# Two halves of a weight tile interleaved element by element, and all large buffers 32 bytes lower

## The chip, the cores and the metric

The kernel runs on one core of one Trainium2 chip. The metric is the device time of one execution in microseconds. Three runs of the kernel before took 1808.83 to 1810.48 us, median 1809.73. A separate execution was profiled; its trace is what the prediction reads.

## The reference, cut to what matters

Two requests of 512 tokens by 1024 features (`x_prompt`, `x_sample`) pass through the same two layers and a last RMSNorm, all in float32. Each layer is `x = x + Mixer(RMSNorm(x))`:

```python
def diff_attention(h, w_in, ..., subln_g, w_out, lambda_init):
    proj = h @ w_in                       # 1024 x 8192
    q, k, v, gate = jnp.split(proj, ...)  # q, k rotated; 16 heads of 128, v: 8 heads of 256
    ...
    p = jax.nn.softmax(s, axis=-1)        # two maps per head
    a = p[:, :, 0] - lam * p[:, :, 1]
    o = rms_norm(a @ v, subln_g, SUBLN_EPS) * (1.0 - lambda_init) * jax.nn.silu(gate)
    return o @ w_out                      # 2048 x 1024

def bidir_retention(h, w_in, ..., subln_g, w_out):
    proj = h @ w_in                       # 1024 x 6144
    q, k, v, gate = jnp.split(proj, ...)  # q, k rotated in pairs; 8 heads of 128, v of 256
    o = rms_norm(o_f + o_b, subln_g, SUBLN_EPS) * jax.nn.silu(gate)
    return o @ w_out
```

`o_f` and `o_b` are decayed, unnormalised attention forwards and backwards in time. Most of the work is in `h @ w_in` of the two layers.

## The kernel before

**Precision by two halves.** A float32 operand is split into a high part (a cast to `fp32r`, made by ScalarE, `hi_of`, the operation at L400) and a low part (the operand minus its high part, made by VectorE, `lo_of`, L403). A product is then three matmuls into the same PSUM bank: high by high, high by low, low by high (`PASSES`).

**Projections.** `h @ w_in` is computed unit by unit, a unit being 256 columns of the weight matrix. Each unit uses a scheme with seven block products (`P1` to `P7`, in the order `SEQ`) instead of eight. For each, `prep` takes blocks of the weights (`raw`, loaded by DMA) or sums of such blocks (`st`, L558), splits them into halves in the ring `ws`, and `product` multiplies them by a prepared operand `Bop` that stands in the buffers `b..` and in slots of one large buffer, `arena`. There are two kinds of unit:

- *pair* (q, k and gates): the weights are the stationary operand, 128 columns at a time; the moving operand has 512 columns. One product is 12 matmuls (four row blocks by three passes, L599). Its two halves stand in one `ws` tile of 1024 elements per partition, the high half in the first 512, the low half in the last 512.
- *wide* (v): the weights are the moving operand, 256 columns; the halves stand in two `ws` tiles (L609).

The ring `ws` has seven places. `projections` prepares products as far ahead of the one that is multiplied as the ring has places for (a pair product takes one, a wide one two). What the products leave in PSUM is combined, rotated or gated, split again and stored to DRAM scratch.

**Mixers and output.** Attention (scores L1116, exponentials L1134, transposes L1161, the product with v L1181) and retention (L1315, L1339, L1359, L1367) load these back. The output product (`out_step`, L891) has its own halves of weights in `ws`; its steps are mixed among the mixers' ones, and the second layer's first output products among the projections.

**Order.** All operations are recorded with a cost and their dependences in `Plan`, which then lays them out: the queue of each engine (PE, ACT = ScalarE, DVE = VectorE, POOL = GpSimd, SP) is in the order in which they would start by these costs. Dependences go by buffer or by part of a buffer. Semaphore waits are added afterwards by the framework, by the memory that operations touch.

**Places in SBUF.** Four pools follow each other in each partition: small tiles (`sm`, each rounded up to 32 bytes), large buffers and tables (`cp`), the arena (`ar`), the rings (`wk`). `view` sends every tile whose size is no multiple of 16 elements to `sm`. So the size of `sm` sets where all that follows begins. In the kernel before, the buffers `b..` begin at 32 modulo 256 bytes, the slots of the arena at 32, 96 or 160 (`shift` of 0, 16 or 32 elements), the rings at 224. In every matmul but the transposes and warming ones, weights and moving operand differ by 64 or 192 modulo 256.

**Constants.** `mhalf` (four times -0.5) and `minus1` (one -1.0) are exponents for GpSimd's power operation: `mhalf` in `norm_cols` (L823), `row_norm`, `x_norm` (L1018); `minus1` for the reciprocals in `combine` (L1144).

The lines that the change is about, as they stand before (L574 to L581):

```python
if self.wide:
    a, b = ws_t([P, 4, n]), ws_t([P, 4, n])
    hi, lo = ((lambda: a.t), a), ((lambda: b.t), b)
else:
    s = ws_t([P, 2, 4, n])
    hi, lo = ((lambda: s[:, 0]), (s, 0)), ((lambda: s[:, 1]), (s, 1))
hi_of(4 * n, lambda: self.like(hi[0]()), src[0], [src[1]], [hi[1]])
lo_of(4 * n, lambda: self.like(lo[0]()), src[0], lambda: self.like(hi[0]()), [src[1], hi[1]], [lo[1]])
```

Of the kernel before, what the change touches and what calls it, by code (L numbers as in the profile page):

```python
# [12 lines left out]
ALU = mybir.AluOpType  # L13
AX = mybir.AxisListType

P = 128
# [3 lines left out]
NT = S // P  # L20
# [233 lines left out]
def trunk_kernel(  # L254
# [7 lines left out]
    nc = tc.nc  # L262
# [4 lines left out]
    sm = ctx.enter_context(tc.tile_pool(name="sm", bufs=1))  # L267
# [12 lines left out]
    def view(pool, tag, i, size, shape, dt=F32):  # L280


        if size % 16 and pool in (cp, wk):
            pool = sm
        if (tag, i) not in places:
            places[tag, i] = pool.tile([P, size], F32, tag=f"{tag}{i}", name=f"{tag}_{i}", bufs=1)
        n = math.prod(shape[1:])
        t = places[tag, i][0:shape[0], 0:n]
        if dt != F32:
            t = t.bitcast(dt)  # L290
        if len(shape) == 3:
            t = t.rearrange("p (a b) -> p a b", a=shape[1])
        elif len(shape) == 4:
            t = t.rearrange("p (a b c) -> p a b c", a=shape[1], b=shape[2])
        return t

    def work(tag, shape, bufs, dt=F32, name=None):
        size = SIZE.get(tag, shape[1])
        return Buf(plan, tag, bufs, lambda i: view(wk, tag, i, size, shape, dt))
# [24 lines left out]
    def const(shape, tag, dt=F32, size=None):  # L324
        return Buf(plan, tag, 1, lambda i: view(cp, tag, i, size or math.prod(shape[1:]), shape, dt))

    def ws_t(shape):
        return work("ws", shape, WS_BUFS, F32R)
# [4 lines left out]
    def st_t(shape, name="st"):  # L333
        return work("st", shape, 3, name=name)
# [13 lines left out]
    def col(n=1, tag="col", bufs=4):  # L348
        return work(tag, [P, n], bufs)
# [18 lines left out]
    def act(n, fn, r, w):  # L368
        plan.op("ACT", 0.1 + 0.00083 * n, fn, r, w)

    def dve(n, fn, r, w, wait=0.0):
        plan.op("DVE", 0.07 + 0.00104 * n, fn, r, w, wait=wait)

    def axpy(n, fn, r, w):

        plan.op("DVE", 0.13 + 0.00104 * n, fn, r, w)

    def pool(n, fn, r, w):
        plan.op("POOL", 0.15 + 0.0024 * n, fn, r, w)

    def evac(n, out, src, scale, r, w, each=0.00115):

        def fn(e):
            if e == "ACT":
                nc.scalar.activation(out(), src(), AF.Copy, scale=scale())  # L385
            else:
                nc.vector.tensor_scalar(out(), src(), scale(), None, op0=ALU.mult)
        plan.op(dict(DVE=0.07 + each * n, ACT=0.1 + 0.00092 * n), 0, fn, r, w)

    def pe(cost, fn, r, w, wait=0.0):  # L390
        plan.op("PE", cost, fn, r, w, wait=wait)

    def dma(out, in_, r, w, kb, eng=None):

        q = eng or nc.sync
        plan.op("SP" if eng is None else "ACT", 0.62, lambda: q.dma_start(out(), in_()), r, w, lands=2.0 + kb / 200.0,
                kb=kb, load=any(isinstance(k[0] if isinstance(k, tuple) else k, Buf) for k in w))

    def hi_of(n, dst, src, r, w):
        act(n, lambda: nc.scalar.copy(dst(), src()), r, w)  # L400

    def lo_of(n, dst, src, hi, r, w):
        dve(n, lambda: nc.vector.tensor_tensor(dst(), src(), hi().bitcast(F32), op=ALU.subtract), r, w)  # L403
# [1 line left out]

    ident = const([P, P], "ident")
    dma(lambda: ident.t, lambda: ident_in, [], [ident], 64, nc.scalar)
    mhalf = const([P, NT], "mhalf")
    dve(4, lambda: nc.vector.memset(mhalf.t, -0.5), [], [mhalf])
    minus1 = const([P, 1], "minus1")  # L410
    dve(1, lambda: nc.vector.memset(minus1.t, -1.0), [], [minus1])
    rows = work("m", [P, P], 4, name="rows")
    gcol = const([P, 28], "gcol")
    dve(1, lambda: nc.vector.memset(gcol[:, 20:21], D * EPS), [], [(gcol, 4)])
# [103 lines left out]
    class Unit:  # L518
# [32 lines left out]
        def prep(self, op):  # L551
            x = self.take
            n = 256 if self.wide else P

            def combine(a, b, fn):
                t = st_t([P, 4, n])
                out = ((lambda: self.like(t.t)), t)
                dve(4 * n, lambda: nc.vector.tensor_tensor(out[0](), a[0](), b[0](), op=fn), [a[1], b[1]], [t])  # L558
                return out
            if op == "P1":  # L560
                src = x(0, 0)
            elif op == "P2":
                src = x(0, 1)
            elif op == "P4":
                src = x(1, 1)
            elif op == "P5":
                src = self.s[1] = combine(x(1, 0), x(1, 1), ALU.add)
            elif op == "P6":
                src = self.s[2] = combine(self.s[1], x(0, 0), ALU.subtract)
            elif op == "P3":  # L570
                src = combine(x(0, 1), self.s[2], ALU.subtract)
            else:
                src = combine(x(0, 0), x(1, 0), ALU.subtract)
            if self.wide:  # L574
                a, b = ws_t([P, 4, n]), ws_t([P, 4, n])
                hi, lo = ((lambda: a.t), a), ((lambda: b.t), b)
            else:
                s = ws_t([P, 2, 4, n])
                hi, lo = ((lambda: s[:, 0]), (s, 0)), ((lambda: s[:, 1]), (s, 1))
            hi_of(4 * n, lambda: self.like(hi[0]()), src[0], [src[1]], [hi[1]])  # L580
            lo_of(4 * n, lambda: self.like(lo[0]()), src[0], lambda: self.like(hi[0]()), [src[1], hi[1]], [lo[1]])  # L581
            self.ops[op] = (hi, lo)
            if op == "P2" and self.early is not None:
                self.early, self.x = None, {}
# [226 lines left out]
    def norm_cols(sq, ps, guard):  # L811

        def fn():
            for t in range(2):
                nc.tensor.transpose(ps[:, t * P:(t + 1) * P], sq[:, t * P:(t + 1) * P], ident.t)
        pe(0.22, fn, [sq, ident], [ps])
        ss, rr = col(2, "css"), col(2, "crr", 9)
        for t in range(2):
            act(P + 120, lambda t=t: nc.scalar.activation(
                ps[:, 256 + t * P:256 + (t + 1) * P], ps[:, t * P:(t + 1) * P], AF.Copy, accum_out=ss[:, t:t + 1]),  # L820
                [(ps, t)], [(ps, 2 + t), (ss, t)])
        guard(ss)
        pool(200, lambda: nc.gpsimd.tensor_tensor(rr.t, ss.t, mhalf[:, 0:2], op=ALU.pow), [ss, mhalf], [rr])  # L823
        return rr

    def new_oT(g):
# [94 lines left out]
    def row_norm(g, t):  # L921

        ss, r = halves.pop((g, t)), col(1, "rsf", 4)
        pool(200, lambda: nc.gpsimd.tensor_tensor(r.t, ss.t, mhalf[:, 0:1], op=ALU.pow), [ss, mhalf], [r])
        return r


# [84 lines left out]
    def x_norm(g, t, late=()):  # L1012
        ss, r = col(1, "ssf", 12), col(1, "rsf", 4)
        jk = slot(16 + t % 2, [P, D])
        x = xnat[g, t]
        act(1250, lambda: nc.scalar.activation(jk.t, x.t, AF.Square, accum_out=ss.t), [x, *late], [jk, ss])
        pool(60, lambda: nc.gpsimd.tensor_scalar(ss.t, ss.t, 1.0 / D, EPS, op0=ALU.mult, op1=ALU.add), [ss], [ss])
        pool(200, lambda: nc.gpsimd.tensor_tensor(r.t, ss.t, mhalf[:, 0:1], op=ALU.pow), [ss, mhalf], [r])  # L1018
        evac(D, lambda: x.t, lambda: x.t, lambda: r.t, [x, r], [x], 0.00058)

    def x_source(layer, tiles, turn):
# [27 lines left out]
    for t in range(NT):  # L1049
        x_norm(1, t, [(Bop['B11', 3], 1)])  # L1050
# [31 lines left out]
    for i in range(2):  # L1082
        dve(16, lambda i=i: nc.vector.tensor_tensor(
            powers[:, :, 2 * i:2 * i + 2], powers[:, :, 2 * i:2 * i + 2], lr[:, i, :].unsqueeze(2).broadcast_to([P, NH, 2]),
            op=ALU.mult), [lr, powers], [powers])
# [52 lines left out]
    def combine(i):  # L1138

        p, sm, n = st[i]['p'], st[i - i % 2]['sm'], i % 2  # L1140
        rc, cc = col(tag="rc"), col(tag="cc")
        on, eng = (pool, nc.gpsimd) if i >= NT else (dve, nc.vector)
        if i >= NT:
            pool(200, lambda: nc.gpsimd.tensor_tensor(rc.t, sm[:, 2 + n:3 + n], minus1.t, op=ALU.pow),  # L1144
                 [(sm, (1, n)), minus1], [rc])
        else:
            dve(2, lambda: nc.vector.reciprocal(rc.t, sm[:, 2 + n:3 + n]), [(sm, (1, n))], [rc])
        on(100, lambda: eng.tensor_scalar(
            cc.t, sm[:, n:n + 1], rc.t, neglam.t, op0=ALU.mult, op1=ALU.mult), [(sm, (0, n)), rc, neglam], [cc])
        axpy(S, lambda: nc.vector.scalar_tensor_tensor(  # L1150
            p[:, 0, :], p[:, 1, :], cc.t, p[:, 0, :], op0=ALU.mult, op1=ALU.add), [p, cc], [p])
        if n:
            pool(40, lambda: nc.gpsimd.tensor_tensor(sm[:, 2:4], sm[:, 0:2], sm[:, 0:2], op=ALU.mult), [sm], [sm])
# [237 lines left out]
    def final_norm(g, t, i, half, n, key, end):  # L1391
# [14 lines left out]
        if not end:  # L1406
            return
        r = row_norm(g, t)
        for h, (z, part) in enumerate(zs):
            if final or h == 0:  # L1410
# [123 lines left out]
```

## Time and profile before

| | |
|---|---|
| runs | 1808.83, 1809.73, 1810.48 us |
| span of the profiled execution | 1807.0 us, 2.7 us under the median of the runs |
| granted TensorE clock | 0.999 of full speed |
| PE busy | 1794.9 us, 10299 matmuls |
| DVE busy | 1477.1 us |
| ACT busy | 895.1 us |
| POOL busy | 169.5 us |
| DMA | 328.81 MB, mean 182 GB/s |

A time outside of the span is what the execution spends before the first and after the last instruction. The stages in the trace: the start and the first layer's projections up to about 635 us, attention to about 1020 us, the second layer's projections to about 1500 us, retention to the end, with overlaps. Matmuls overlap in the array: the mean length of one in a group (392 ns, say) is longer than the distance from one to the next, so lengths of unbroken runs divided by their number of matmuls tell what one costs. `PEld` are the loads of the stationary operand, which run beside matmuls. A group is named by line, engine, operation and `out<-in`; behind the bar stand the busy time, the mean length in ns and the idle time before, with what ended it.

### The profile page before, as it was taken

The numbers are of one execution on the slowest core, as the hardware profiler recorded it, in microseconds if no ns is written. First come the engines' busy times: TensorE is split into PE (matmuls) and PEld (weight loads), VectorE is DVE, ScalarE is ACT, GpSimd is POOL, SyncE is SP. The second block draws the span as 40 slices with busy tenths as digits, with TensorE's granted clock in tenths as the row PEclk, the third lists the DMA queues.
The fourth block names the chain that finished last, engine by engine and source line by source line (L and its number), as shares of the span: only waits on it lengthen the run. The fifth ranks groups of instructions, "written<-read, shape, count | busy, mean of one in ns | idle before, by whom it ended". The sixth has DMA issues, their size and how long they took to land.

```text
span 1807.0 us, 27780 instructions
## 1 busy us (share of the span) xinstructions
PE 1794.9 (99%) x10299; PEld 1558.1 (86%) x10299; DVE 1477.1 (82%) x2319; ACT 895.1 (50%) x1856; POOL 169.5 (9%) x323
## 2 busy tenths in 40 slices
PE   9999999999999999999999999999999999999998
PEld 6789889898988888888888888898989898888887
DVE  7958787778699888888888897787887967888887
ACT  7753444433434565554555866444434355444346
POOL 1000000000000022222322300000000000111113
PEclk9999999999999999999999999999999999999999
DMA  6444455555545685444554524464657559765662
GB/s 217 134 126 137 161 140 178 184 168 155 174 126 175 201 334 198 178 156 159 190 204 140 190 73 146 140 210 146 205 156 228 151 170 396 272 238 182 225 218 94
DMA packets 162767, 328.81 MB, mean 182 GB/s; under 512 B 12724, under 2 KB 76872, under 8 KB 162632
## 3 DMA queue, kind: packets, MB, share of 16 engines
q1 hardware_dynamic: 162304, 326.71, 54.1%
q8 instruction: 81, 1.33, 0.3%
q14 instruction: 54, 0.44, 0.1%
q10 hardware_dynamic: 328, 0.34, 0.1%
HBM read 209.55 MB, written 117.44 MB: 181 GB/s over the span
## 4 chain that ended last, share of the span: by engine, by line
PE 93%; DVE 2%; DMA 2%; ACT 2%; issue 1%; POOL 0%; SPq 0%; POOLq 0%; DVEq 0%; ACTq 0%
PE pj L599 20%; PE pj L891 19%; PE sc L599 10%; PE pj L609 10%; PE o L599 8%; PE o L1181 5%; PE sc L1116 5%; PE sc L609 5%; PE o L609 2%; PE o L1359 2%; PE tp L1161 2%; PE sc L1315 1%; PE o L1367 1%; PE tp L1339 1%; DMA raw<-in_ret_w_out_dram 1%
## 5 line engine op out<-in xcount | busy, mean ns | idle before, releaser
L891 PE MATMUL pj<-ws,arena 128*128 128x512 f32 x1542 | 391.2, 397 | 0.0
L891 PEld LDWEIGHTS pj<-ws,arena 128*128 128x128 f32 x1542 | 277.7, 188 | 52.7
L599 PE MATMUL pj<-b,ws 128*128 128x512 f32 x1080 | 265.0, 392 | 0.0
L599 PEld LDWEIGHTS pj<-b,ws 128*128 128x128 f32 x1080 | 201.4, 188 | 43.0
L403 DVE TENSOR_TENSOR ws<-st,ws 128x512 fp32r<-128x512 f32 (+1 forms) x192 | 147.9, 774 | 74.8 <-ACT ws L400 56.7
L896 DVE SCALAR_TENSOR_TENSOR b<-pj,crr,b 128x512 f32<-128x512 f32 (+1 forms) x257 | 189.9, 744 | 21.4 <-PE pj L891 21.0
L403 DVE TENSOR_TENSOR ws<-raw,ws 128x512 fp32r<-128x512 f32 (+1 forms) x164 | 141.5, 868 | 71.3 <-ACT ws L400 61.0
L400 ACT CAST ws<-st 128x512 fp32r<-128x512 f32 (+1 forms) x192 | 132.4, 693 | 121.4 <-PE pj L599 36.4
L599 PE MATMUL sc<-arena,ws 128*128 128x512 f32 x768 | 186.8, 392 | 0.0
L599 PE MATMUL o<-arena,ws 128*128 128x512 f32 x744 | 180.0, 393 | 1.1 <-ACT m L385 0.6
L599 PEld LDWEIGHTS sc<-arena,ws 128*128 128x128 f32 x768 | 144.0, 188 | 31.3
L400 ACT CAST ws<-raw 128x512 fp32r<-128x512 f32 (+1 forms) x164 | 125.7, 772 | 87.0 <-PE o L599 45.0
L599 PEld LDWEIGHTS o<-arena,ws 128*128 128x128 f32 x744 | 138.4, 188 | 31.7 <-DVE arena L463 1.4
L599 PE MATMUL pj<-arena,ws 128*128 128x512 f32 x648 | 160.3, 392 | 0.4 <-DVE arena L463 0.4
L599 PEld LDWEIGHTS pj<-arena,ws 128*128 128x128 f32 x648 | 120.8, 188 | 26.7 <-DVE arena L463 0.7
L1134 ACT ACTIVATE b<-sc,nm 128x512 f32<-128x512 f32 x128 | 88.0, 689 | 66.9 <-DVE nm L1124 66.5
L636 ACT COPY c<-pj 128x512 f32<-128x512 f32 x104 | 60.9, 586 | 119.7 <-PE pj L599 66.4
L609 PE MATMUL pj<-ws,b 128*128 128x256 f32 x960 | 116.8, 276 | 0.0
L609 PEld LDWEIGHTS pj<-ws,b 128*128 128x128 f32 x960 | 113.2, 188 | 0.7
L1116 PE MATMUL sc<-arena 128*128 128x512 f32 x384 | 101.2, 395 | 0.3 <-ACT b L1134 0.3
L1181 PEld LDWEIGHTS o<-arena 128*128 128x128 f32 x768 | 93.1, 188 | 2.7
L1181 PE MATMUL o<-arena 128*128 128x256 f32 x768 | 93.7, 278 | 0.0
(207 smaller groups left out, 2855.9 us busy)
## 6 DMA issues: line engine op xcount, KB each, us to landing
qk<-os SPq DMA_DIRECT2D x192, 256.0 KB, 3.6
arena<-qk SPq DMA_DIRECT2D x96, 512.0 KB, 5.8
raw<-in_da_w_in_dram SPq DMA_DIRECT2D x64, 512.0 KB, 5.1
v<-os SPq DMA_DIRECT2D x64, 512.0 KB, 4.3
arena<-v SPq DMA_DIRECT2D x64, 512.0 KB, 4.1
raw<-in_ret_w_in_dram SPq DMA_DIRECT2D x48, 512.0 KB, 4.8
os<-g SPq DMA_DIRECT2D x32, 512.0 KB, 7.4
g<-e SPq DMA_DIRECT2D x48, 256.0 KB, 4.6
```

Of the source, the lines that this page charges most:

```text
L400: act(n, lambda: nc.scalar.copy(dst(), src()), r, w)
L403: dve(n, lambda: nc.vector.tensor_tensor(dst(), src(), hi().bitcast(F32), op=ALU.subtract), r, w)
L599: nc.tensor.matmul(ps.t, a[u][0]()[:, k, :], bt[k][:, v, :], start=(opens and k == 0 and i == 0), stop=(k == 3 and i == 2), skip_group_che ...
L609: nc.tensor.matmul(ps[:, (t % 2) * 256:(t % 2) * 256 + 256], bt[k][:, v, t * P:(t + 1) * P], a[u][0]()[:, k, :], start=(opens and t % 2 == ...
L636: act(S, lambda c=c, ps=ps: nc.scalar.copy(c.t, ps.t), [ps], [c])
L891: nc.tensor.matmul(ps[:, here], o[a][:, e, t * P:(t + 1) * P], u[b][:, e, here], start=(m == 0), stop=(m == 5))
L896: axpy(n, lambda half=half, here=here, ps=ps: nc.vector.scalar_tensor_tensor(half, ps[:, here], rr[:, t % 2:t % 2 + 1], half, op0=ALU.mult ...
L1116: nc.tensor.matmul(s.t, q[:, a, t * P:(t + 1) * P], k[:, b, :], start=(n == 0), stop=(n == 2))
L1134: act(840, lambda j=j, s=s, m=m: nc.scalar.activation(p[:, j, :], s.t, AF.Exp, bias=m.t, accum_out=sm[:, 2 * j + n:2 * j + n + 1]), [s, m] ...
L1161: nc.tensor.transpose(tp[:, j * P:(j + 1) * P], p[:, 0, j * P:(j + 1) * P], ident.t)
L1181: nc.tensor.matmul(o[:, e * 256:(e + 1) * 256], v[b][:, j, e * P:(e + 1) * P], aT[a][:, j, :], start=(n == 0), stop=(n % 12 == 11), skip_g ...
L1359: nc.tensor.matmul(o[:, e * 256:(e + 1) * 256], v_[v][:, 2 * c + j, e * P:(e + 1) * P], a_[:, u, j * 256:(j + 1) * 256], start=(e == 0 and ...
```

## The change

The two halves of a pair product's weights stay in one `ws` tile, but element by element: high, low, high, low. Each half is then written, subtracted from and loaded into the array with a step of two elements (8 bytes). Wide products, the output products and the mixers keep their layout.

`minus1` becomes the fifth column of `mhalf`. Its own tile of 32 bytes in `sm` goes, and so every tile behind it begins 32 bytes lower: the buffers `b..` at 0 modulo 256, the slots of the arena at 0, 64 or 128, the rings at 192. The differences among them stay. The power operations name the part of `mhalf` that they read.

```diff
-    mhalf = const([P, NT], "mhalf")
-    dve(4, lambda: nc.vector.memset(mhalf.t, -0.5), [], [mhalf])
-    minus1 = const([P, 1], "minus1")
-    dve(1, lambda: nc.vector.memset(minus1.t, -1.0), [], [minus1])
+    mhalf = const([P, NT + 1], "mhalf")
+    dve(4, lambda: nc.vector.memset(mhalf[:, 0:NT], -0.5), [], [(mhalf, 0)])
+    dve(1, lambda: nc.vector.memset(mhalf[:, NT:NT + 1], -1.0), [], [(mhalf, 1)])
...
-                s = ws_t([P, 2, 4, n])
-                hi, lo = ((lambda: s[:, 0]), (s, 0)), ((lambda: s[:, 1]), (s, 1))
+                s = ws_t([P, 4, n, 2])
+                hi, lo = ((lambda: s[:, :, :, 0]), (s, 0)), ((lambda: s[:, :, :, 1]), (s, 1))
...
-        pool(200, lambda: nc.gpsimd.tensor_tensor(rr.t, ss.t, mhalf[:, 0:2], op=ALU.pow), [ss, mhalf], [rr])
+        pool(200, lambda: nc.gpsimd.tensor_tensor(rr.t, ss.t, mhalf[:, 0:2], op=ALU.pow), [ss, (mhalf, 0)], [rr])
...
-            pool(200, lambda: nc.gpsimd.tensor_tensor(rc.t, sm[:, 2 + n:3 + n], minus1.t, op=ALU.pow),
-                 [(sm, (1, n)), minus1], [rc])
+            pool(200, lambda: nc.gpsimd.tensor_tensor(rc.t, sm[:, 2 + n:3 + n], mhalf[:, NT:NT + 1], op=ALU.pow),
+                 [(sm, (1, n)), (mhalf, 1)], [rc])
```

More of the change, by code (lines that the diff above doesn't have):

```diff
@@ L923, in row_norm @@
         ss, r = halves.pop((g, t)), col(1, "rsf", 4)
-        pool(200, lambda: nc.gpsimd.tensor_tensor(r.t, ss.t, mhalf[:, 0:1], op=ALU.pow), [ss, mhalf], [r])
+        pool(200, lambda: nc.gpsimd.tensor_tensor(r.t, ss.t, mhalf[:, 0:1], op=ALU.pow), [ss, (mhalf, 0)], [r])
         return r
@@ L1017, in x_norm @@
         pool(60, lambda: nc.gpsimd.tensor_scalar(ss.t, ss.t, 1.0 / D, EPS, op0=ALU.mult, op1=ALU.add), [ss], [ss])
-        pool(200, lambda: nc.gpsimd.tensor_tensor(r.t, ss.t, mhalf[:, 0:1], op=ALU.pow), [ss, mhalf], [r])
+        pool(200, lambda: nc.gpsimd.tensor_tensor(r.t, ss.t, mhalf[:, 0:1], op=ALU.pow), [ss, (mhalf, 0)], [r])
         evac(D, lambda: x.t, lambda: x.t, lambda: r.t, [x, r], [x], 0.00058)
```

## The prediction

> **What bounds the kernel now.** I read the page first, then the chain that ended last piece by piece, then the pieces in which PE stands still, and last the single instruction forms that the change touches. The first lines are the page's.
>
> ```profile
> span 1807.0 us, 27780 instructions
> PE 1794.9 (99%) x10299; PEld 1558.1 (86%) x10299; DVE 1477.1 (82%) x2319; ACT 895.1 (50%) x1856; POOL 169.5 (9%) x323
> PE 93%; DVE 2%; DMA 2%; ACT 2%; issue 1%; POOL 0%; SPq 0%; POOLq 0%; DVEq 0%; ACTq 0%
> ```
>
> PE is busy 99% of the span and makes 93% of the chain. "Busy" hides how dense the matmuls are, so I take lengths of unbroken runs from the chain (start, length, what):
>
> ```profile
> 75.27 8.24 PE pj L599 x36
> 185.37 5.44 PE pj L609 x48
> ```
>
> 36 matmuls of 512 columns (pair products, L599) take 8.24 us, 228.9 ns each; 48 of 256 columns (wide products, L609) take 5.44 us, 113.3 ns each. PE idles on almost nobody: the view of PE's own waits has 8 rows, of which these are the first and the last.
>
> ```profile
> PE sc L1010 <- DVE minus L411: 1.4, 1, 1.4
> PE tp L815 <- DVE b L403: 0.2, 1, 0.2
> ```
>
> So the time moves only in three ways: the length of a matmul changes, the short stretches where PE does wait get longer, or an engine beside PE becomes slow enough to starve it. The pair products are these matmuls (groups by shape):
>
> ```profile
> L599 PE MATMUL pj<-b,ws 128*128 128x512 f32 x1080 | 265.0, 392 | 0.0
> L599 PE MATMUL sc<-arena,ws 128*128 128x512 f32 x768 | 186.8, 392 | 0.0
> L599 PE MATMUL o<-arena,ws 128*128 128x512 f32 x744 | 180.0, 393 | 1.1 <-ACT m L385 0.6 <-DVE arena L463 0.3
> L599 PE MATMUL pj<-arena,ws 128*128 128x512 f32 x648 | 160.3, 392 | 0.4 <-DVE arena L463 0.4
> L599 PE MATMUL sc<-b,ws 128*128 128x512 f32 x120 | 29.1, 391 | 0.0
> L891 PE MATMUL pj<-ws,arena 128*128 128x512 f32 x1530 | 389.8, 398 | 0.0
> L1116 PE MATMUL sc<-arena 128*128 128x512 f32 x384 | 101.2, 395 | 0.3 <-ACT b L1134 0.3
> ```
>
> The five L599 groups hold 3360 matmuls, 280 products of 12. One nanosecond on each is 3.36 us, 0.19% of the time. I call 0.2% (3.6 us) the limit below which a measurement of this kernel can't tell a change from none.
>
> **The change part by part.** The order of instructions on every engine stays as it is; what changes is addresses, steps and some waits.
>
> *Weight loads of pair products.* They now step over 8 bytes instead of 4. Two questions: does a load still hide, and does it disturb the matmul that streams beside it? The first restart of PE after the wait at 50 us shows a bare load (timeline of PEld, two loads merged; one load lasts 188 ns by its line's row):
>
> ```profile
> 50.27 0.30 PEld L599 LDWEIGHTS o<-arena,ws 128*128 128x128 f32 x2 [0.57 <-DVE arena L463]
> L599 PEld LDWEIGHTS pj<-b,ws x1080: 187/188/192, 55.7 to 1509.6; 128*128 128x128 f32 x180
> ```
>
> Two loads end 0.30 us after the first began, and each lasts 0.19, so the second began 0.11 us after the first: a load keeps PE for 0.11 us at most. Beside a 228.9 ns matmul it may double, to 0.22, before anything is late. The wide matmul at 113.3 ns is barely longer than a load, but wide products keep their contiguous layout. [...]
>
> For the second question I looked for 512-column matmuls with no load beside them, the last ones ahead of a wait (first two rows), against the run of all (third):
>
> ```profile
> L599 PE MATMUL sc<-arena,ws x1: 397/397/397, 45.1 to 45.1; 128*128 128x512 f32 x1
> L1116 PE MATMUL sc<-arena x1: 388/388/388, 647.5 to 647.5; 128*128 128x512 f32 x1
> L599 PE MATMUL pj<-b,ws x1080: 388/392/481, 55.9 to 1509.8; 128*128 128x512 f32 x180
> ```
>
> Alone they take 388 and 397 ns, with a load beside them 392 in the median. The load does not lengthen the stream today, so a load with another step has no collision to remove. I take 0 for PE. The ends that I keep: minus 2.2 and plus 5.0 ns per matmul (rivals A and B).
>
> *Writes and reads of the halves.* ACT writes the high half with an 8-byte step (L400), DVE reads it and writes the low half with that step (L403). No write of that step is in the trace, but reads are: the second layer's projections read raw weights by parity. Between 1377 and 1430 us all `raw` casts of 128x512 are such (x5), and `st` is read contiguously:
>
> ```profile
> L403 DVE TENSOR_TENSOR ws<-st,ws 128x512 fp32r<-128x512 f32 x8 | 5.4, 687 | 2.9 <-ACT ws L400 2.9
> L403 DVE TENSOR_TENSOR ws<-raw,ws 128x512 fp32r<-128x512 f32 x5 | 3.3, 684 | 1.3 <-ACT ws L400 1.3
> L403 DVE TENSOR_TENSOR ws<-raw,ws 128x1024 fp32r<-128x1024 f32 x2 | 2.4, 1217 | 0.0
> L400 ACT CAST ws<-st 128x512 fp32r<-128x512 f32 x8 | 4.9, 621 | 3.6 <-PE pj L599 2.1 <-issue 1.5
> L400 ACT CAST ws<-raw 128x512 fp32r<-128x512 f32 x5 | 3.2, 660 | 6.7 <-PE o L599 5.4 <-PE pj L609 1.3
> ```
>
> DVE doesn't notice (684 against 687), ACT pays 39 ns. For the unseen write I take 39 ns on both. The ends: 0, and half rate, which is 512 elements more, 1217-684 = 533 ns. Below nothing I find no reason. ACT: 280 x 39 ns = 10.9 us on an engine with 912 us idle. DVE: 10.9 us on one with 330 us idle. Both lie under PE except where PE waits for them, which is the start:
>
> ```profile
> 20.00:50.20 30.20, 28.37 (x136) 22.31 (x134) 29.72 (x49) 25.00 (x46) 4.08 (x6) 1.00 0.32 102
> 20.00:470.00 450.00, 448.10 (x2588) 391.69 (x2587) 357.39 (x543) 215.03 (x356) 4.08 (x6) 1.00 0.50 151
> L403 DVE TENSOR_TENSOR ws<-b,ws 128x512 fp32r<-128x512 f32 x5 | 3.2, 676 | 0.0
> L403 DVE TENSOR_TENSOR ws<-st,ws 128x512 fp32r<-128x512 f32 x4 | 2.7, 674 | 0.0
> L403 DVE TENSOR_TENSOR ws<-raw,ws 128x512 fp32r<-128x512 f32 x2 | 1.4, 678 | 0.0
> ```
>
> (Windows: length, then PE, PEld, DVE, ACT, POOL busy.) From 20 to 50.2 us DVE is busy 29.72 of 30.20 us and the chain runs through it; 11 low halves of pair products are made there. 11 x 39 ns = **0.4 us** on the path. At half rate it is 11 x 533 = 5.9 us. In the whole first projection (20 to 470) DVE has 93 us free.
>
> [...]
>
> *Waits.* An interleaved tile spreads its high half over its whole ring place. Where that place held a wide tile, the high half had overlapped only its first two row blocks, and ACT could start while the wide product still read the rest; now it waits for the whole. That concerns 24 places in the run, with two casts each, such as these (timeline of ACT):
>
> ```profile
> 190.05 1.14 ACT L400 CAST ws<-st 128x512 fp32r<-128x512 f32 x2
> 198.26 1.14 ACT L400 CAST ws<-raw 128x512 fp32r<-128x512 f32 x2 [1.30 <-PE pj L609]
> ```
>
> The casts move by six 256-column matmuls, 6 x 113.3 ns = 0.68 us. Queued behind them on ACT are copies out of PSUM and casts of later tiles, for which DVE and then PE wait. Seven ring places stand for some six products of 2.75 us (12 x 228.9 ns), so these weights are wanted over 10 us later; ACT idles 235 us of that stage, and PE's waits have no row of such a place. Cost 0; if nothing covered it, 24 x 0.68 = 16.3 us. The low halves of these places had waited for the last matmul already, so DVE's own wait just goes.
>
> *Addresses.* Every large buffer and ring lies 32 bytes lower: multiples of 64, where all were 32 off. The offsets between weights and moving data stay (64 or 192 modulo 256). No matmul of the trace starts on a multiple of 64, so the cost is unseen; I take 0, the nearest rows being the matmuls of three different offsets (L599 moving at 32, L1116 at 96, L891 at 224 modulo 256), with medians or means from 392 to 398 ns. *Constants:* two memsets as before, and Pool's 60 powers read another address: 0.
>
> The sum: 0 + 0.4 + 0 + 0 = 0.4 us on the profiled span of 1807.0. The median 1809.73 lies 2.7 us above that span, outside of it. **Forecast: 1810.1 us**, own range 1806.5 to 1813.5.
>
> **The rivals.**
>
> A, *faster: boundaries.* A 512-column matmul takes 228.9 ns, two of 256 take 226.7. If the missing 2.2 ns is a piece of memory that straddles because data starts 32 off a multiple of 64, the new base removes it from L599, L891 and L1116: 5274 x 2.2 ns = 11.6 us, 1798.1 us. For it: three unlike address pairs have the same price, so something common makes it. Against: the 256-column matmuls start just as far off, and no per-matmul charge shows there.
>
> B, *slower: the load's step disturbs PE.* [...] The price is the nearest disturbed matmul (timeline of PE; each run lasts until the next one starts):
>
> ```profile
> 1504.42 0.87 PE L1315 MATMUL sc<-arena 128*128 128x256 f32 x6
> 1505.13 1.57 PE L1359 MATMUL o<-arena 128*128 128x256 f32 x12
> 1506.55 0.87 PE L1367 MATMUL o<-arena,b 128*128 128x256 f32 x6
> ```
>
> 0.71/6 and 1.42/12 are 118.3 ns where 113.3 is the run above: 5.0 ns. 3360 x 5.0 = 16.8 us, 1826.5 us. It decides from 1.1 ns per matmul on. For it: nothing in the trace loads weights with a step. Against: the matmuls alone are no shorter. A load beyond twice its 0.11 us would cost more still, and lies outside my range. [...]
>
> C, *slower: strided writes at half rate.* 5.9 us at the start and, if a third of the uncovered 16.3 us of the 24 places comes out as well, 5.4 us there: 1809.7 + 11.3 = 1821.0 us. Against: the reads show no such thing on DVE.
>
> D, *the change doesn't do what it says* (steps folded away): not so, the built instructions carry the 8-byte step; its time would be 1809.7.
>
> **How the numbers follow.** The forecast with D 0.45; A and its like 0.23; B 0.20; C 0.12. So same 0.45, faster 0.23, slower 0.32. The range reaches to A with 4 us below it, and to B with 8 us above, since B's price may be larger: 1794 to 1834, leaving about 0.2 out.
>
> **What would show it.** Right: 36 L599 matmuls in a row still 8.24 us; L403 on `ws` within 40 ns of 684; ACT's casts on `ws` near 660; PE's list of waits as short. A: that run at 8.16 us, L891 and L1116 shorter too. B: that run at 8.42 us while L609 stays at 5.44. C: L403 on `ws` near 1217 ns and DVE near 1620 us busy. I am wrong altogether if PE's run lengths move by over 1 ns per matmul.

## The result: 23.5 us slower, and the profile after

The changed kernel takes 1833.12 us (median of four runs, 1832.16 to 1834.24), the kernel before 1809.61 beside it (1808.83 to 1810.48). The ratio is 1.013, with a 95% interval of 1.0117 to 1.0143. The profiled spans are 1807.0 and 1832.3 us. The forecast was 1810.1 with a range of 1794 to 1834; what came has the sign and the place of rival B, but pair products lost less than it priced, and wide products, which it had left alone, lost the rest. Lines behind the merged constants are one lower now: L599 is L598, L609 is L608, L891 is L890, L1116 is L1115.

The page of the kernel after, its first line, engines, and shares of the chain that ended last:

```profile
span 1832.3 us, 27771 instructions
PE 1819.4 (99%) x10299; PEld 1592.9 (87%) x10299; DVE 1478.3 (81%) x2319; ACT 904.7 (49%) x1856; POOL 171.4 (9%) x323
PE 95%; ACT 1%; DVE 1%; issue 1%; DMA 1%; POOL 0%; SPq 0%; POOLq 0%; ACTq 0%
```

PE has the same 10299 matmuls and is busy 24.5 us longer; the span is 25.3 us longer. No other engine gained anything like that: DVE 1.2, ACT 9.6, POOL 1.9 us. So PE did not begin to wait for somebody, its matmuls take longer. The chain of the kernel after tells which (start, length, what):

```profile
77.22 8.40 PE pj L598 x36
...
158.86 5.46 PE pj L608 x48
...
167.12 5.65 PE o L608 x48
172.77 5.65 PE sc L608 x48
...
189.73 5.66 PE pj L608 x48
```

36 pair matmuls take 8.40 us where they took 8.24: 233.3 ns each, 4.4 more. The wide products, whose code the change leaves alone, take 5.65 us where they took 5.44: 117.7 ns, also 4.4 more. One wide run of these, the first, is still at 5.46. Taking all distances from one matmul to the next in the trace, the pair products sum to 789.7 us after 774.3 (+15.4), the wide ones to 316.2 after 305.7 (+10.5), and all the rest to 0.6 less: together the 25.3. The other large groups did not move (groups by shape of the kernel after):

```profile
L890 PE MATMUL pj<-ws,arena 128*128 128x512 f32 x1530 | 389.8, 398 | 0.0
...
L598 PE MATMUL pj<-b,ws 128*128 128x512 f32 x1080 | 269.4, 396 | 0.0
...
L1115 PE MATMUL sc<-arena 128*128 128x512 f32 x384 | 101.3, 395 | 0.3 <-ACT b L1133 0.3
```

The pair group's mean goes from 392 to 396 ns, L890 stays at 398 and L1115 at 395. About 1.5 us of the 25.3 belong to this one execution and not to the kernel (the first experiment, with the same layout, has a span of 1830.8): its window from 20 to 50.2 us has a granted clock of 0.94 (the column behind POOL), where before it had 1.00, and seven pair matmuls there lie 427 ns apart, 1.4 us too much in all. The run of 36 begins at 77.22; in the first experiment it begins at 75.44.

The window's row (length, then PE, PEld, DVE, ACT, POOL busy):

```profile
20.00:50.20 30.20, 28.45 (x130) 23.08 (x129) 28.27 (x45) 23.84 (x43) 4.70 (x6) 0.94 0.28 98
```

Last, the casts. Groups by shape of the kernel after, between 1377 and 1430 us as before:

```profile
L403 DVE TENSOR_TENSOR ws<-st,ws 128x512 fp32r<-128x512 f32 x8 | 5.4, 687 | 3.1 <-ACT ws L400 3.1
L400 ACT CAST ws<-st 128x512 fp32r<-128x512 f32 x8 | 5.2, 660 | 3.6 <-PE pj L598 2.1 <-issue 1.5
L400 ACT CAST ws<-raw 128x512 fp32r<-128x512 f32 x5 | 3.2, 666 | 4.0 <-PE pj L608 2.1 <-PE o L598 1.4 <-PE sc L608 0.5
```

DVE's subtraction is at 687 ns as before; ACT's cast of `st` went from 621 to 660, exactly the 39 ns that were taken, and the cast whose source was strided already went from 660 to 666.

### The profile page after: what moved, and what is told of

Its sections match the earlier page's. It is cut to its first block, busy times and chain, and to the rows that moved or that the text cites. A ratio compares the mean times of both kernels' runs of the same rounds, so it can differ in the third digit from the quotient of the medians.

```text
span 1832.3 us, 27771 instructions
## 1 busy us (share of the span) xinstructions
PE 1819.4 (99%) x10299; PEld 1592.9 (87%) x10299; DVE 1478.3 (81%) x2319; ACT 904.7 (49%) x1856; POOL 171.4 (9%) x323
## 4 chain that ended last, share of the span: by engine, by line
PE 95%; ACT 1%; DVE 1%; issue 1%; DMA 1%; POOL 0%; SPq 0%; POOLq 0%; ACTq 0%
PE pj L598 21%; PE pj L890 18%; PE sc L598 11%; PE pj L608 10%; PE o L598 9%; PE sc L608 5%; PE o L1180 5%; PE sc L1115 5%; PE o L608 2%; PE o L1358 2%; PE tp L1160 2%; PE sc L1314 1%; PE o L1366 1%; PE tp L1338 1%; ACT c L914 0%
## 5 line engine op out<-in xcount | busy, mean ns | idle before, releaser
L890 PE MATMUL pj<-ws,arena 128*128 128x512 f32 x1542 | 391.2, 397 | 0.0
L890 PEld LDWEIGHTS pj<-ws,arena 128*128 128x128 f32 x1542 | 277.7, 188 | 52.7
L598 PE MATMUL pj<-b,ws 128*128 128x512 f32 x1080 | 269.4, 396 | 0.0
L598 PEld LDWEIGHTS pj<-b,ws 128*128 128x128 f32 x1080 | 209.1, 195 | 39.9
L400 ACT CAST ws<-st 128x512 fp32r<-128x512 f32 (+1 forms) x192 | 138.7, 727 | 136.4 <-PE pj L598 38.9
L598 PE MATMUL sc<-arena,ws 128*128 128x512 f32 x768 | 190.2, 396 | 0.0
L598 PE MATMUL o<-arena,ws 128*128 128x512 f32 x744 | 184.7, 399 | 0.9 <-ACT m L385 0.6
L598 PEld LDWEIGHTS sc<-arena,ws 128*128 128x128 f32 x768 | 149.5, 195 | 29.2
L598 PEld LDWEIGHTS o<-arena,ws 128*128 128x128 f32 x744 | 144.6, 196 | 29.7 <-DVE arena L462 0.9
L598 PE MATMUL pj<-arena,ws 128*128 128x512 f32 x648 | 163.1, 396 | 0.4 <-DVE arena L462 0.3
L598 PEld LDWEIGHTS pj<-arena,ws 128*128 128x128 f32 x648 | 125.5, 195 | 24.9 <-DVE arena L462 0.6
L608 PE MATMUL pj<-ws,b 128*128 128x256 f32 x960 | 120.9, 281 | 0.0
L608 PEld LDWEIGHTS pj<-ws,b 128*128 128x128 f32 x960 | 117.1, 189 | 0.6
L1115 PE MATMUL sc<-arena 128*128 128x512 f32 x384 | 101.3, 395 | 0.3 <-ACT b L1133 0.3
```

What stands on the lines that cost most here:

```text
L598: nc.tensor.matmul(ps.t, a[u][0]()[:, k, :], bt[k][:, v, :], start=(opens and k == 0 and i == 0), stop=(k == 3 and i == 2), skip_group_che ...
L608: nc.tensor.matmul(ps[:, (t % 2) * 256:(t % 2) * 256 + 256], bt[k][:, v, t * P:(t + 1) * P], a[u][0]()[:, k, :], start=(opens and t % 2 == ...
L890: nc.tensor.matmul(ps[:, here], o[a][:, e, t * P:(t + 1) * P], u[b][:, e, here], start=(m == 0), stop=(m == 5))
L1115: nc.tensor.matmul(s.t, q[:, a, t * P:(t + 1) * P], k[:, b, :], start=(n == 0), stop=(n == 2))
```

## The experiments

Four parts of the change can be parted: the strided load, the strided write, the addresses, and what the wide products have to do with any of it. The theories were: the load's step lengthens the pair matmuls and wide products take the pace over (called P); a wide product slows for another reason, such as its address; or the whole comes from the addresses. Where the rows of two kernels stand for their paces, they are the run of 36 pair matmuls near 75 us and runs of 48 wide ones between 150 and 200 us, in the chain that ended last.

### Interleaving alone, the addresses of before

```diff
-                s = ws_t([P, 2, 4, n])
-                hi, lo = ((lambda: s[:, 0]), (s, 0)), ((lambda: s[:, 1]), (s, 1))
+                s = ws_t([P, 4, n, 2])
+                hi, lo = ((lambda: s[:, :, :, 0]), (s, 0)), ((lambda: s[:, :, :, 1]), (s, 1))
```

> The halves interleaved, all addresses as before. Theory L (the 8-byte step of the weight load sets a slower pace, which the wide products behind it inherit): all of the loss is here, 1830 to 1836 us, pair matmuls 233.3 ns apart, wide ones 117.7. Theory A (the new base addresses do it): 1809 to 1811 us, 228.9 and 113.3. Theory W (strided writes of ACT and DVE disturb PE's reads): as L in time.

1832.7 us (1832.65 to 1835.19), ratio 1.0134 (1.0117 to 1.0151): the whole loss. The chain has the changed kernel's runs:

```profile
75.44 8.40 PE pj L599 x36
...
157.09 5.46 PE pj L609 x48
165.35 5.65 PE o L609 x48
```

The slow stretch of the kernel after is not in this execution: the ten loads from 27.08 us on take 2.18 us, there 3.56, from 27.87 on. Its pair run at 75.44 begins 0.17 us after that of before; writes and waits cost little at the start, if anything.

### Addresses and constants alone

The diff of the change without the two lines above.

> The constants in one tile and so all buffers 32 bytes lower, weights in two contiguous halves. Theory L and theory W: 1808 to 1811 us, 228.9 and 113.3 ns. Theory A: 1830 us or more. If both parts have a share, for example wide products slow by their address and pair products by the step, about 1820 us.

1809.74 us (1808.06 to 1814.76, ten runs) against 1808.87 (1808.34 to 1814.49, nineteen runs), ratio 1.0004 (0.9995 to 1.0013): nothing.

```profile
74.31 8.24 PE pj L598 x36
...
168.31 5.44 PE sc L608 x48
```

### Strided load alone

Halves are written as before; only the views that the products load step over 8 bytes. The values then are a mixture of both halves.

```diff
-            self.ops[op] = (hi, lo)
+            if not self.wide:
+                flat = lambda: s.t.rearrange("p a k n -> p (a k n)")
+                self.ops[op] = (((lambda: flat().rearrange("p (k n a) -> p k n a", k=4, a=2)[:, :, :, 0]), hi[1]),
+                                ((lambda: flat().rearrange("p (k n a) -> p k n a", k=4, a=2)[:, :, :, 1]), lo[1]))
```

> Addresses of before; halves written contiguously as before, but the pair products load their weights with an 8-byte step out of the same tile, so that they multiply a mixture of both halves. Theory L: as the interleaved kernel, 1830 to 1836 us. Theory W: 1809 to 1811 us.

1832.15 us (1831.6 to 1832.63), ratio 1.0126 (1.0111 to 1.0141). The load alone makes the loss. Summing distances between matmuls, the pair products lose 13.6 us here (787.9 after 774.3) and the wide ones 10.5 (316.2).

```profile
75.23 8.40 PE pj L604 x36
...
156.86 5.46 PE pj L614 x48
165.12 5.65 PE o L614 x48
```

### Strided write alone

Halves are written interleaved; the products load contiguous runs, a mixture again.

```diff
-                s = ws_t([P, 2, 4, n])
+                s = ws_t([P, 4, n, 2])
...
+                flat = lambda: s.t.rearrange("p k n a -> p (k n a)")
+                self.ops[op] = (((lambda: flat().rearrange("p (a k n) -> p a k n", a=2, k=4)[:, 0]), hi[1]),
+                                ((lambda: flat().rearrange("p (a k n) -> p a k n", a=2, k=4)[:, 1]), lo[1]))
```

> Addresses of before; halves written element by element (ACT and DVE with an 8-byte step, DVE's read too), but loaded contiguously, so that the products use a mixture of both halves. Theory L: 1809.5 to 1811 us, with 0.1 to 0.5 us for slower casts at the start. Theory W: 1830 us or more.

1809.78 us (1808.91 to 1815.1, ten runs), ratio 1.0003 (0.9994 to 1.0013): the write costs nothing, though ACT's casts are long (groups by shape of this kernel, 1377 to 1430 us):

```profile
L400 ACT CAST ws<-st 128x512 fp32r<-128x512 f32 x8 | 5.2, 657 | 4.4 <-DVE e L676 2.1 <-issue 1.7 <-PE pj L614 0.7
```

The profiled execution is the rare one of 1815.1 us (before has one of 1814.49 in nineteen), and it shows something of use. Its chain, in the first layer's projections and in the second's:

```profile
75.21 8.24 PE pj L604 x36
...
155.31 5.66 PE pj L614 x48
163.73 5.65 PE o L614 x48
...
1184.81 5.47 PE o L614 x48
1190.28 5.44 PE sc L614 x48
```

With loads as in the kernel before and pair products at 8.24, all wide products of the first layer run at 5.65 and those of the second at 5.44. The wide sum is 311.4 us, 5.7 over that of before, which is what this execution lost; the other nine, at 1808.91 to 1810.8 us, have no room for such a loss. So a wide matmul has two paces, 113.3 and 117.7 ns, with the same instructions and addresses. What put the first layer of this execution on the slower one is not shown.

### A transpose ahead of wide products

In the changed kernel, one transpose of the identity (128 columns) before the first tile's matmuls of `P1` and `P2` of each wide unit.

```diff
+                elif op in ("P1", "P2") and t == 0:
+                    nc.tensor.transpose(ps[:, 0:P], ident.t, ident.t)
```

> The changed kernel, with one transpose of the identity (128 columns, into a part of the bank that the first matmul clears) ahead of products P1 and P2 of each wide unit. Theory P (a run of wide products keeps the pace with which it begins, and transposes bring it back): the run of 240 that P2 opens and the run of P1 go at 113.3 ns instead of 117.7; about 8 x 280 x 4.4 ns = 9.8 us less, against 15 transposes of 0.11 to 0.15 us, so 1824 to 1827 us. Rival R (the step, or what stands in the buffers, slows the wide products all the time): 117.7 ns stays and the transposes add 1.6 to 2.3 us, 1834 to 1836 us.

1826.05 us (1824.99 to 1827.3), ratio to before 1.0095 (1.0078 to 1.0112): some 7 us come back from the 23.5.

```profile
75.07 8.40 PE pj L598 x36
...
156.71 5.46 PE pj L610 x48
165.09 5.46 PE o L610 x48
170.54 5.44 PE sc L610 x48
...
195.11 5.66 PE pj L610 x48
```

The runs behind a transpose, and those that follow them without a pair product between, are at 5.44 again. The one that comes after a pair product without a transpose (195.11) is at 5.66. The wide sum falls from 316.2 to 308.4 us, pair runs stay at 8.40. That is what P says: 7.8 of the wide products' 10.5 us go when something else stands ahead of a run, though its own instructions and addresses are the same. In the changed kernel itself, the same can be read in its second layer, where transposes stand between two pieces of a wide run (chain of the kernel after):

```profile
1187.82 1.42 PE pj L608 x12
1189.23 0.44 PE tp L715 x4
1189.67 4.11 PE pj L608 x36
1193.78 2.80 PE pj L598 x12
1196.58 5.65 PE o L608 x48
```

12 matmuls behind a pair product take 118 ns each, the 36 behind four transposes 114, and the next run behind a pair product 117.7 again.

### A load with a step of 16 bytes

Writes contiguous, loads of pair products at every fourth element; the products use a mixture.

```diff
+                self.ops[op] = (((lambda: flat().rearrange("p (k n a) -> p k n a", k=2, a=4)[:, :, :, 0]), hi[1]),
+                                ((lambda: flat().rearrange("p (k n a) -> p k n a", k=2, a=4)[:, :, :, 1]), lo[1]))
...
-                            ps.t, a[u][0]()[:, k, :], bt[k][:, v, :], start=(opens and k == 0 and i == 0),
+                            ps.t, a[u][0]()[:, k % 2, :], bt[k][:, v, :], start=(opens and k == 0 and i == 0),
```

> Addresses and writes of before; pair products load weights with a step of four elements (16 bytes), out of the same tile, so that they use a mixture of its values. [...]

1846.29 us (1845.8 to 1848.52), ratio 1.0207 (1.0191 to 1.0222).

```profile
79.00 8.64 PE pj L604 x36
...
182.46 5.44 PE pj L614 x48
```

Pair matmuls take 240.0 ns, yet the wide runs behind them are back at 113.3; only the first, behind transposes, takes 5.66. So not every disturbed load leaves the slow wide pace behind. The lengths of one load (min, median, max; the line's own rows, of the kernel after and then of this one) stand beside 187/188/192 of before:

```profile
L598 PEld LDWEIGHTS pj<-b,ws x1080: 193/194/198, 57.2 to 1535.6; 128*128 128x128 f32 x180
```

```profile
L604 PEld LDWEIGHTS pj<-b,ws x1080: 307/309/334, 58.4 to 1549.6; 128*128 128x128 f32 x180
```

A load grows by 6 ns at 8 bytes and by 121 at 16, roughly the 0.11 us that a bare load keeps PE. So a step of 16 bytes does not cost what one of 8 bytes does: 240.0 ns per pair matmul and 1846.29 us, where the strided load of 8 bytes alone has 233.3 ns and 1832.15 us. What makes the difference is not shown, and the last four kernels speak against a price by the step alone.

### Strided load of the low half alone

Only the low half's loads, one in three, step over 8 bytes; the low half's values are a mixture.

```diff
+                self.ops[op] = ((hi[0], hi[1]),
+                                ((lambda: flat().rearrange("p (k n a) -> p k n a", k=4, a=2)[:, :, :, 1]), lo[1]))
```

> Addresses and writes of before; only the low half's loads, one of three, have the 8-byte step, so that one pass of three uses a mixture of values. If the cost goes by stepped loads: a third, 1.5 ns per pair matmul, 5 us, with the wide products on top only if they start late: 1814 to 1818 us, or up to 1825 with slow wide products. If one stepped load in three is enough for the slow pace of all: 1830 to 1834 us.

1826.59 us (1825.97 to 1828.26), ratio 1.0097 (1.0082 to 1.0112).

```profile
75.03 8.32 PE pj L604 x36
...
164.15 5.65 PE o L614 x48
```

A third of the loads costs half of the pair products' loss: 8.32 is 0.08 over 8.24, where all loads make 0.16. In the trace the matmuls during which a strided load runs lie 235.6 ns apart in the mean, the others 229.3. The wide products are as slow as with all loads strided (sum 316.1 us). The price is not proportional to the number of strided loads, and the time lies 1.6 us above 1825, the highest that was expected of a proportional price.

### Rings 64 bytes lower, halves contiguous

The kernel before, with a shorter arena, so that weights begin 128 bytes from the moving operand modulo 256, instead of 192.

```diff
-    arena = ar.tile([P, 18 * 1024 + 80], F32R, tag="arena", name="arena")
+    arena = ar.tile([P, 18 * 1024 + 64], F32R, tag="arena", name="arena")
```

> The kernel before with all rings 64 bytes lower (160 modulo 256), so that weights and moving operand of the pair and wide products differ by 128 instead of 64 or 192. If addresses play no part in PE's pace: 1808 to 1811 us, 228.9 and 113.3 ns. If the offset of the two streams matters: 1 to 5 ns on each pair matmul, 1813 to 1826 us.

1837.11 us (1836.84 to 1837.27), ratio 1.0153 (1.0138 to 1.0168). A move of the rings by 64 bytes, without any stride, costs more than the whole change, and more than the 1813 to 1826 us that were expected if the offset matters.

```profile
75.47 8.37 PE pj L599 x36
...
165.27 5.69 PE o L609 x48
```

So a load's step is not the only thing that sets the pace of the stream; where the two operands begin does so too (232.5 ns per pair matmul after 228.9). Matmuls whose operands both lie in the arena, which did not move, lengthen here as well: L1181 sums to 89.7 us after 88.4, L1359 to 45.3 after 43.7. So not all of the 28 us is paid by the matmuls whose offset changed, which points to a part played by what runs beside or ahead of a group. The last four kernels vary offset and step.

### Two more offsets, each with contiguous and with interleaved halves

To find the room, the constants are merged as in the change, `gcol` has 24 columns instead of 28, and the arena is 64 bytes longer (offset 0) or 128 (offset 64; there the ring `ssf` of small tiles has ten places instead of twelve). By the offset of pair products, weights minus moving operand modulo 256, the kernel before has 192. In wide products the roles are exchanged, so their offset is 256 minus that.

```diff
-    arena = ar.tile([P, 18 * 1024 + 80], F32R, tag="arena", name="arena")
+    arena = ar.tile([P, 18 * 1024 + 96], F32R, tag="arena", name="arena")
...
-    gcol = const([P, 28], "gcol")
+    gcol = const([P, 24], "gcol")
```

> Halves contiguous as before; the small tiles are packed 64 bytes closer and the arena is 64 bytes longer, so that weights and moving operand of the products begin at the same place modulo 256 (before: 192 apart; with the rings 64 lower: 128 apart). Instructions as before. Theory offset (the pace depends on how far weights and moving operand are apart modulo 256, and 0 is like 128): pair products 232.4 ns, wide 119.0 ns, as with the rings 64 lower, about 1837 us. Rival (only 128 is bad): pair 229.0 and wide 113.3 to 117.7, 1809 to 1820 us.

> The kernel of the run before this one (offset 0), with the halves of pair products interleaved. Theory step (the load's step of 8 bytes costs what it costs wherever the tiles lie): pair products 4.3 ns longer than in the twin with contiguous halves, plus 14 us on the pair products and 0 to 10 us on the wide ones. Rival (the step collides only at the offset of 192 that the kernel had): pair products within 1 ns of the twin's, total within 5 us of it.

> As the kernel with offset 0, contiguous halves, but the arena 128 bytes longer and one ring of small tiles two places shorter, so that weights begin 64 bytes behind the moving operand modulo 256 in pair products, and 192 in wide ones: the two offsets of the kernel before, exchanged. Theory offset, 64 and 192 alike: pair 229.0 ns, wide 113.3 to 113.7, 1809 us. Rival (each offset has its own price): the pair products at some other pace between 226.7 and 233 ns, 1802 to 1823 us; below 1806 us it would be a faster kernel than before.

> The kernel with offset 64, with the halves of pair products interleaved. Theory step: pair products 4.3 ns longer than in its contiguous twin, plus 14 us, and 0 to 10.5 us on the wide ones: 1823 to 1835 us if the twin takes 1809. Rival (the step collides only at the offset of 192): within 5 us of the twin.

Chains of the four, in this order:

```profile
75.00 8.16 PE pj L598 x36
...
162.81 5.75 PE o L608 x48
168.56 5.76 PE sc L608 x48
```

```profile
75.57 8.40 PE pj L598 x36
...
171.48 5.76 PE sc L608 x48
```

```profile
77.40 8.40 PE pj L598 x36
...
167.49 5.65 PE o L608 x48
```

```profile
75.23 8.28 PE pj L598 x36
...
155.71 5.66 PE pj L608 x48
164.14 5.44 PE o L608 x48
```

The third execution starts late (77.40), as that of the kernel after does (77.22). In the last one the first wide run, the one behind transposes, is the slow one (5.66), and those behind pair products are fast (5.44): a transpose does not make a run fast as such. All of it in one table (us for 36 pair and for 48 wide matmuls, and the median time):

| offset | contiguous | interleaved |
|---|---|---|
| 192 | 8.24, 5.44: 1809 | 8.40, 5.65: 1833 |
| 128 | 8.37, 5.69: 1837.11 | not run |
| 0 | 8.16, 5.76: 1826.65 (1825.79 to 1827.75), ratio 1.0095 (1.0078 to 1.0112) | 8.40, 5.76: 1844.72 (1844.71 to 1844.97), ratio 1.0195 (1.0175 to 1.0214) |
| 64 | 8.40, 5.65: 1839.88 (1839.33 to 1841.82), ratio 1.0169 (1.0152 to 1.0187) | 8.28, 5.44: 1818.81 (1818.57 to 1819.01), ratio 1.0051 (1.0035 to 1.0067) |

At offset 192 the step costs 4.4 ns per pair matmul, at 0 it costs 6.7, and at 64 it *saves* 3.3 ns and brings the wide products back to 113.3: 1818.8 against 1839.9 us. The theory that the step has a price of its own is wrong, and so is the rival that only the offset of 192 collides. The two contiguous kernels missed what was expected too: 0 is not like 128, since pair products are shorter and wide ones longer, and 64 is not like 192; it lies beyond the rival's 1823 us. In totals, summing distances between matmuls again: the contiguous kernel at 0 saves 5.6 us on the pair products, loses 17.1 on the wide ones and 3.0 on the output products, whose offsets move too.

The place of one operand alone does not decide. The kernel before and the one with the rings lower have the same moving operand; the kernel before and the contiguous ones at 0 and 64 have the rings at the same place; yet all four differ. The output products give a second look. Their moving operand is in the rings and their weights in the arena, 128 bytes (modulo 256) behind the moving operand of the pair products. So their own offset is 192 in the kernel before, 0 with the rings lower, and 128 and 64 in the contiguous kernels that the table calls 0 and 64. By the same distances they sum to 362.1, 361.4, 365.1 and 365.7 us. That is the order of the pair products at these offsets (0, 192, 128, 64 from short to long), though each pair of operands lies at other places. It points to the distance and not to the places; part of it may be taken over from the groups around.

None of the other six forms beats that of the kernel before.

## Why the prediction was wrong where it was

**Weight loads: the step that failed.** "The load does not lengthen the stream today, so a load with another step has no collision to remove. I take 0 for PE." The strided load alone makes the loss, +14.9 us by rows on the pair products (3360 x 0.16/36; 13.6 by summed distances) and 10.5 on the wide ones. By the prediction's own sign, "I am wrong altogether if PE's run lengths move by over 1 ns per matmul", it fails: they moved by 4.4. The first half of the sentence is refuted too: with the same loads at offset 0 the run of 36 takes 8.16 us instead of 8.24. So 2.2 of the 228.9 ns of before were already a matter of where the operands of load and stream lie. The evidence had been three lengths of matmuls, 388 and 397 ns alone and 392 together. Two lone matmuls that differ by 9 ns can't exclude an effect of 2 to 4 ns, lone matmuls don't have the spacing of a run, and the lengths of 388 to 392 ns overlap the next matmul, so they are no measure of a pace of 229. What the prediction asked of a load, that it hides, was right (it grew by 6 ns, with over 100 to spare by an estimate, 228.9 ns less 0.11 us) and was the wrong question. A load's length in the profile did grow with the step: little at 8 bytes (194 ns after 188), much at 16 (309).

**Rival B** named the mechanism's place and sign, and a price of 5.0 ns, where 4.4 was measured. That the two are close is luck: the 5.0 came from 256-column matmuls of retention, and the L1359 row that it took is not the pace of its group, whose distances sum to 43.7 us for 384 matmuls, 113.9 ns each. The term that it lacked is the wide products: "while L609 stays at 5.44" was wrong, they went to 5.65. With that term, 1809.7 + 14.9 + 10.5 = 1835.1 us, 2 us from what came. That 1833.1 lies within the range, 0.9 us below its end, is luck as well: the 8 us above B were kept for a larger price of B, and what filled them were the wide products, which no rival had. That a load's 8-byte step as such slows PE is not borne out: at offset 64 the run of 36 is shorter with that step (8.28 us after 8.40).

**Rival A** had the size right by chance. Its run of 8.16 us exists, at offset 0, but not for the reason given: moving both operands down by 32 bytes, to multiples of 64, left 8.24 (addresses alone).

**Writes and reads of the halves.** 39 ns were taken for both engines; ACT pays 39 (621 to 660), DVE nothing (687). On the path 0.4 us were forecast. The run of 36 begins 0.17 us later with interleaving alone (75.44 after 75.27) and 0.06 earlier with strided writes alone (75.21); single executions differ by more (74.31 with the addresses alone), and the strided write alone shows no difference in time. C is out.

**Waits.** Cost 0, as forecast. PE's own waits in the kernel after have no row for a late `ws`, and sum to 5.8 us after 4.8; first and last of nine rows:

```profile
PE sc L1009 <- DVE mhalf L410: 1.4, 1, 1.4
PE o L598 <- DVE arena L462: 0.2, 1, 0.2
```

**Addresses and constants.** 0 was right, ratio 1.0004. But "matmuls of three different offsets" with one price misled: those were places of single operands, and what the experiments point to is how far the two lie apart, which the change kept.

**Not settled.** The runs show that step and offset together change the pace, and that a wide run at offset 64 or 192 keeps one of two paces (113.3 or 117.7 ns). That it is the distance and not the pair of places is argued from the output products; both operands were moved together by 32 bytes only. To count the distance modulo 256 is the author's choice; the runs do not test it against another. What makes the pace change is not shown: the hardware profile has starts and lengths, no account of the operands' reads. Nor is it shown what puts a wide run on the slower pace: transposes ahead make it fast in the changed kernel (5.46) and slow at offset 64 interleaved (5.66), and one of ten executions with strided writes lost 5.7 us on wide products that the others kept. A kernel with pair products at offset 0 (8.16) and wide ones at 192 (5.44) would, by these rows, gain 3360 x 2.2 ns = 7.4 us, an estimate that leaves out what one group takes over from another. Both use the ring `ws`, so it needs another layout; it wasn't tried.

## What to carry to other kernels

Here TensorE is busy 99% of the span, and nanoseconds per matmul decide on a layout of weights (4.4 on each of the 3360 pair matmuls make 14.9 us). In such a kernel ask not only whether a load still hides but whether the stream beside it keeps its pace, and read that from unbroken runs, not from single matmuls. The interleaving had no fixed price: per pair matmul it cost 4.4 ns at offset 192, cost 6.7 at 0 and saved 3.3 at 64. So try such a change at two or three offsets before it is judged. And look at the groups that the change does not touch: here two fifths of the loss (10.5 of 25.3 us) lay there.

## What the runs showed of the hardware that was not expected

- With contiguous loads, a run of 36 matmuls of 512 columns went at 226.7, 228.9, 232.5 and 233.3 ns where the two operands' addresses lay 0, 192, 128 and 64 apart modulo 256. A common shift of both by 32 bytes changed nothing (ratio 1.0004); larger ones were not run.
- A run of 48 matmuls of 256 columns at offset 64 or 192 went at 113.3 or at 117.7 ns (5.44 or 5.65 us). A transpose ahead changed which (5.65 to 5.44 us for 48 in the changed kernel), but one execution with strided writes had its first layer at 117.7, for a reason that no run shows. The pace was kept through the five runs of 48 that follow each other between two pair products (5.44 to 5.47 us in the kernel before, 5.65 to 5.66 in the one after).
- A load of 128 weights took 188 ns in the profile at a step of 4 bytes, 194 at 8 and 309 at 16 (medians).
- With the 8-byte step ACT's cast of `st` to 512 columns took 660 ns after 621, DVE's subtraction 687 as before.
